# Retention input projections of row groups two to four by Strassen's seven half-block products

## The chip, the cores and the metric

The kernel runs on one core of a Trainium2 chip. The metric is device time in microseconds of one execution. Five engines work side by side from their own instruction queues: TensorE (PE; its weight loads are listed as PEld), VectorE (DVE), ScalarE (ACT), GpSimd (POOL) and SyncE (SP), which here issues every DMA. Matrix products read SBUF and accumulate in PSUM banks of 128 x 512 float32.

## The reference, cut to what matters

A decoder trunk of two layers over 2048 tokens of width 1024 in float32: one gated retention layer, then one sliding-window attention layer whose keys and values come from the residual stream after the first.

```python
def retention_layer(x, g_norm, w_in, w_out, sin, cos):
    proj = rmsnorm(x, g_norm) @ w_in                 # 1024 -> 1024 + 1024 + 2048 + 2048
    q, k, v, gate = jnp.split(proj, [D_MODEL, 2 * D_MODEL, 2 * D_MODEL + RET_V_TOTAL], axis=-1)
    q = theta_shift(q.reshape(b, s, RET_HEADS, RET_QK_DIM), sin, cos)
    k = theta_shift(k.reshape(b, s, RET_HEADS, RET_QK_DIM), sin, cos)
    v = v.reshape(b, s, RET_HEADS, RET_V_DIM)
    o = rms(retention(q, k, v))                      # chunks of 128, state 256 x 512 per head
    o = o.reshape(b, s, RET_V_TOTAL) * jax.nn.silu(gate)
    return x + o @ w_out

def step(state, inp):                                # inside retention, one chunk
    scores = jnp.einsum('bihd,bjhd->bhij', qc, kc) * intra_decay[None]
    intra = jnp.einsum('bhij,bjhe->bihe', scores, vc)
    inter = jnp.einsum('bihd,bhde->bihe', qc, state) * q_decay[None, :, :, None]
    new_state = state * chunk_decay + jnp.einsum('bjhd,bjhe->bhde', kc * k_decay, vc)
```

The attention layer then computes shared keys and values, gated attention with sinks and a bias by distance, and its output product.

## The kernel before

**Precision.** Every large product is made of three matmuls: each operand is split into a rounded high part (type fp32r, ACT) and the rest (DVE), and high x high, high x low and low x high are added in PSUM. `wload` (L100) brings a 128 x 1024 piece of weights through three rotating buffers `raw`, casts it (`whi`, L114) and subtracts (`wlo`, L116: DVE in the retention layer, POOL in the attention layer).

**Tiling.** Tokens are taken in four row groups of 512 (`T`), with four heads each: 16 units `(g, h)`, in this order. `main(u)` makes the projections of a unit from the group's split rows `xhi`, `xlo`, by three calls of `proj` (L119): queries and keys together (feature-major, 512 columns of tokens), values, gate. Each runs over eight blocks of 128 features for four PSUM banks, and all four banks of the pool `pp` turn over at its end (`evac_qk` rotates by position, `evac_v` splits the values, `evac_g` applies the gate). `ret(u)` runs four chunks of retention: scores (`sc_r`, L351), transposed keys (`kt_r`), state update (`dl_r`, L388 to L390), output (`o_r`), normalising and gating, transposing back (`ot_r`). The states of the four heads stay in SBUF (`S32`). `out_a(u)` multiplies a unit's output with its rows of the output weights in eight feature blocks (`pp_ao`) and adds them to the group's residual rows `x1`, which stay in SBUF for the group's four heads (L444), and are stored to `xmid` with the last head.

**Order.** The loop before `phase_b` interleaves `main(u + 1)` with `ret(u)` (`drive`, two steps to one), then emits `out_a(u)`. The order of emission is the priority; a scheduler orders the instructions of each engine before the run, pulling ready work forward into gaps. At run time each queue is strictly in order: an instruction that waits holds up what stands behind it, on SP too.

**Around it.** `row_stats` gets the scales of a group's rows, which are applied to the values and inside the norm and not to the rows. `bias_rows` (L204 on, run once after unit 0's projections) makes the bias by distance for 16 heads and stores 128 copies of each to `bdr` in DRAM (L216). `prep` brings rows to the attention layer. That layer's output product `out_b` loads each residual block, adds and stores it (`res`, L680 to L682).

Of the kernel before, what the change touches and what calls it, by code (L numbers as in the profile page):

```python
# [12 lines left out]
F32 = mybir.dt.float32  # L13
# [3 lines left out]
ALU = mybir.AluOpType  # L17
# [37 lines left out]
def tile_yoco(ctx, tc, x, x_t, w_a, wo_a, w_kv, w_b, wo_b, ag, kvg, bg, kng, qng,  # L55
# [8 lines left out]
    xtp = ctx.enter_context(tc.tile_pool(name="xtp", bufs=2))  # L64
# [13 lines left out]
    # the first function's table, loaded while the first rows come in  # L78
# [8 lines left out]

    def bank(name, tag="rr"):
# [11 lines left out]
    def wload(src, cols, name, kscale=None, key=None):  # L100
        """A piece of weights, split. Its rows scaled: in its first use, which stores it."""
# [17 lines left out]
    def proj(src, nk, xhi, xlo, feat, evac, name, kscale=None, key=None, cols=512, before=None):  # L119
        kn = 1024 // cols  # L120
        bk = [pp.tile([P, 512], F32, tag="pp", name=f"pp_{name}_{m}") for m in range(4)]
# [26 lines left out]
    def xt_tiles(name):  # L148
        mk = lambda hl, j: xtp.tile([P, KT // 2, T], F32R, tag=f"x{hl}", name=f"x{hl}_{name}_{j}")
        return [mk("hi", 0), mk("hi", 1)], [mk("lo", 0), mk("lo", 1)]  # L150

    def row_stats(g):
        """Mean squares + eps of the rows of a group, [P, MT], and their roots' inverses."""
        ss = small.tile([P, MT], F32, tag="ssx", bufs=2, name=f"ssx_{g}")
        r = small.tile([P, MT], F32, tag="rx", bufs=2, name=f"rx_{g}")
        for m in range(MT):
            xin = wp.tile([P, D], F32, tag="raw", bufs=3, name=f"xin_{g}_{m}")
            nc.sync.dma_start(xin, x[(g * MT + m) * P : (g * MT + m + 1) * P, :])
            junk = small.tile([P, D], BF16, tag="junk", bufs=1, name=f"jx_{g}_{m}")
            nc.scalar.activation(junk, xin, AF.Square, accum_out=ss[:, m : m + 1])  # L160
            if m == MT - 1:
                nc.gpsimd.tensor_scalar(ss, ss, 1.0 / D, EPS, op0=ALU.mult, op1=ALU.add)
                nc.gpsimd.tensor_tensor(r, ss, neghalf[:, :MT], op=ALU.pow)
            yield ss, r

    def stats(g, tiles, tag):
        """The scales of a group's rows, in every partition: [P, T]."""
# [16 lines left out]
    def prep(g, rb):  # L184
        """The normalised, transposed rows of a group, split."""
        xhi, xlo = xt_tiles(f"b{g}")
        for kp in range(KT // 2):
# [3 lines left out]
            hi, lo = (t[kp // 2][:, kp % 2 * 2 : kp % 2 * 2 + 2, :] for t in (xhi, xlo))  # L191
# [10 lines left out]
    bdr = dram.tile([QH, P, 384], F32, name="bdr")  # L202

    def bias_rows():  # L204
        """Bias by distance, a one-hot product; a copy for each query row, so that
        rows 384 wide read at a stride of 383 give bias[i, head, j]."""
# [5 lines left out]
        bp = pp.tile([P, 512], F32, tag="pp", name="biasp")  # L212
# [3 lines left out]
        nc.sync.dma_start(bdr, bsb.unsqueeze(1).to_broadcast([QH, P, 384]))  # L216
# [3 lines left out]
    # ------------------------------------------------------------ retention layer  # L220
    def phase_a(pa):
        cst = pa["const"]
        p1, p2, vp, gp = pa["p1"], pa["p2"], pa["v"], pa["g"]
# [9 lines left out]

        def main(u):
            g, h = units[u]
            n = f"a{u}"
            if h == 0:
                xt = xt_tiles(n)

# [614 lines left out]
```

## Time and profile before

| | |
|---|---|
| time, median of 3 runs | 2584.8 us (2583.43 to 2589.42) |
| span of the profiled execution, first to last instruction | 2580.5 us |
| mean granted TensorE clock | 0.990 |
| bytes moved by DMA | 283.29 MB, mean 110 GB/s |
| retention layer, its first to its last projection or output product | about 8 to 1737 us |

The profile is one execution of the program, and its span leaves out what lies before the first and behind the last instruction. A group of instructions carries its line, engine, operation, output and inputs, shapes and count, then its busy time and the mean duration of one in ns, then the idle time of the engine ahead of it with what ended that idle time. Matmuls overlap, so that their durations add up to more than the time they take.

### The profile page before, as it was taken

The numbers are of one execution on the slowest core, as the hardware profiler recorded it, in microseconds if no ns is written. First come the engines' busy times: TensorE is split into PE (matmuls) and PEld (weight loads), VectorE is DVE, ScalarE is ACT, GpSimd is POOL, SyncE is SP. The second block draws the span as 40 slices with busy tenths as digits, with TensorE's granted clock in tenths as the row PEclk, the third lists the DMA queues.
The fourth block names the chain that finished last, engine by engine and source line by source line (L and its number), as shares of the span: only waits on it lengthen the run. The fifth ranks groups of instructions, "written<-read, shape, count | busy, mean of one in ns | idle before, by whom it ended". The sixth has DMA issues, their size and how long they took to land.

```text
span 2580.5 us, 31642 instructions
## 1 busy us (share of the span) xinstructions
PE 2513.0 (97%) x12098; PEld 2046.3 (79%) x12098; DVE 1490.4 (58%) x2653; ACT 1017.3 (39%) x1859; POOL 487.0 (19%) x429
## 2 busy tenths in 40 slices
PE   8699999999999999999999999989999999999998
PEld 6588888888888888888888888878767777877887
DVE  4255455454555545546455454567876677777766
ACT  4242333333324333233333332334544454555553
POOL 1000000020000020000002000033325364363350
PEclk9899999999999999999999999999999999999999
DMA  5532223243223243222324222227332342333323
GB/s 173 106 115 82 90 81 116 85 141 114 80 81 110 85 155 106 82 82 82 123 74 143 90 74 82 86 90 255 126 122 91 131 142 83 139 124 113 127 102 107
DMA packets 92228, 283.29 MB, mean 110 GB/s; under 512 B 10763, under 2 KB 17068, under 8 KB 92076
## 3 DMA queue, kind: packets, MB, share of 16 engines
q1 hardware_dynamic: 92076, 281.27, 32.3%
q8 instruction: 95, 1.56, 0.2%
q14 instruction: 57, 0.47, 0.1%
HBM read 242.43 MB, written 38.80 MB: 109 GB/s over the span
## 4 chain that ended last, share of the span: by engine, by line
PE 89%; DVE 4%; DMA 3%; issue 2%; ACT 1%; POOL 1%; SPq 0%; POOLq 0%; ACTq 0%; DVEq 0%
PE pp_ao L136 4%; PE pp_ao L138 4%; PE pp_ao L137 4%; PE o_t L663 2%; PE s_t L626 2%; PE pp_bo L136 2%; PE pp_bo L138 2%; PE pp_bo L137 2%; PE pT_t L647 2%; DMA raw_a1qk<-in_w_a 1%; PE sc_r L351 1%; PE ot_r L422 1%; PE dl_r L388 1%; PE dl_r L389 1%; PE o_r L398 1%
## 5 line engine op out<-in xcount | busy, mean ns | idle before, releaser
L94 POOL TENSOR_SCALAR r_o_r<-sso_r,es_a 128x1 f32<-128x1 f32 x64 | 30.6, 478 | 1288.0 <-ACT jo_r L416 1288.0
L136 PE MATMUL pp_ao<-ohi_r,whi_ao 128*128 128x512 f32 x512 | 203.3, 400 | 0.0
L137 PE MATMUL pp_ao<-olo_r,whi_ao 128*128 128x512 f32 x512 | 202.6, 396 | 0.0
L116 DVE TENSOR_TENSOR wlo_ao<-raw_ao,whi_ao 128x1024 fp32r<-128x1024 f32 x64 | 78.4, 1225 | 211.1 <-ACT whi_ao L114 210.8
L138 PE MATMUL pp_ao<-ohi_r,wlo_ao 128*128 128x512 f32 x512 | 199.5, 396 | 0.0
L637 ACT ACTIVATE P_t<-P_t,nm_t 128x256 f32<-128x256 f32 (+1 forms) x256 | 127.5, 499 | 144.6 <-DVE nm_t L629 143.6
L114 ACT CAST whi_ao<-raw_ao 128x1024 fp32r<-128x1024 f32 x64 | 67.1, 1048 | 192.4 <-PE pp_ao L137 53.7
L629 DVE CUSTOM_DVE_ANT_0 P_t<-s_t,bias,nsnk 128x256 f32<-128x256 f32 (+1 forms) x256 | 114.9, 469 | 32.6 <-PE s_t L626 31.9
L138 PEld LDWEIGHTS pp_ao<-ohi_r,wlo_ao 128*128 128x128 f32 x512 | 96.4, 188 | 22.9
L137 PEld LDWEIGHTS pp_ao<-olo_r,whi_ao 128*128 128x128 f32 x512 | 96.5, 188 | 22.7 <-issue 0.2
L136 PEld LDWEIGHTS pp_ao<-ohi_r,whi_ao 128*128 128x128 f32 x512 | 96.7, 189 | 22.4 <-issue 0.2
L468 ACT CAST Shi_r<-S 128x512 fp32r<-128x512 f32 x120 | 70.4, 618 | 109.2 <-PE o_r L398 65.7
L409 DVE SCALAR_TENSOR_TENSOR S<-S,dl_r 128x512 f32<-128x512 f32 x112 | 73.2, 682 | 61.3 <-PE dl_r L390 61.2
L626 PE MATMUL s_t<-kst,qst_b 128*128 128x256 f32 (+1 forms) x512 | 100.5, 297 | 6.1 <-DVE nm_t L629 4.6
L626 PEld LDWEIGHTS s_t<-kst,qst_b 128*128 128x128 f32 x512 | 82.8, 192 | 29.7 <-DVE nm_t L629 7.4
L469 DVE TENSOR_TENSOR Slo_r<-S,Shi_r 128x512 fp32r<-128x512 f32 x120 | 78.1, 686 | 38.0 <-ACT Shi_r L468 37.8
L643 DVE TENSOR_SCALAR P_t<-P_t,den_t 128x256 f32<-128x256 f32 (+1 forms) x256 | 92.7, 425 | 1.9
L136 PE MATMUL pp_bo<-ohi_t,whi_bo 128*128 128x512 f32 x224 | 88.7, 401 | 3.6 <-DVE gate_b L590 3.6
L137 PE MATMUL pp_bo<-olo_t,whi_bo 128*128 128x512 f32 x224 | 88.2, 394 | 0.0
L116 POOL TENSOR_TENSOR wlo_bo<-raw_bo,whi_bo 128x1024 fp32r<-128x1024 f32 x28 | 71.1, 2542 | 86.5 <-ACT whi_bo L114 64.5
L138 PE MATMUL pp_bo<-ohi_t,wlo_bo 128*128 128x512 f32 x224 | 86.4, 394 | 0.0
L416 ACT ACTIVATE jo_r<-o_r 128x512 bf16<-128x512 f32 x64 | 38.0, 593 | 101.5 <-PE o_r L401 101.3
(867 smaller groups left out, 7308.0 us busy)
## 6 DMA issues: line engine op xcount, KB each, us to landing
raw_ao<-in_wo_a SPq DMA_DIRECT2D x64, 512.0 KB, 3.2
res<-xmid SPq DMA_DIRECT2D x56, 256.0 KB, 2.8
raw_bo<-in_wo_b SPq DMA_DIRECT2D x28, 512.0 KB, 3.2
xin<-in_x SPq DMA_DIRECT2D x16, 512.0 KB, 3.6
xraw_b<-xmid SPq DMA_DIRECT2D x16, 512.0 KB, 3.4
xmid<-res SPq DMA_DIRECT2D x32, 256.0 KB, 2.6
xraw_a<-in_x_t SPq DMA_DIRECT2D x12, 512.0 KB, 3.2
x_r<-in_x_t SPq DMA_DIRECT2D x12, 512.0 KB, 5.3
```

The lines of the kernel that those rows point to most:

```text
L114: nc.scalar.copy(hi, raw)
L116: eng.tensor_tensor(lo, raw, hi.bitcast(F32), op=ALU.subtract)
L136: nc.tensor.matmul(o, hi[:, kk, sl], xh, start=st, stop=False)
L137: nc.tensor.matmul(o, hi[:, kk, sl], xl, start=False, stop=False)
L138: nc.tensor.matmul(o, lo[:, kk, sl], xh, start=False, stop=sp)
L409: nc.vector.scalar_tensor_tensor(S32[h][:, d, :], S32[h][:, d, :], gamC[h], dl[d], op0=ALU.mult, op1=ALU.add)
L468: nc.scalar.copy(hi, S32[h][:, d, :])
L469: nc.vector.tensor_tensor(lo, S32[h][:, d, :], hi.bitcast(F32), op=ALU.subtract)
L626: nc.tensor.matmul(o, qst[m][:, h, :], kst[:, kv * 2 + hl, kb + b0 : kb + 2, :], start=hl == 0, stop=hl == 1)
L629: nc.vector.tensor_tensor_reduce(out=pt[:, j, :w], in0=o, in1=bias[:, kv * GQ + h, b0 * P :], scale=-1.0, scalar=nsv[:, h : h + 1], op0=AL ...
L637: nc.scalar.activation(pt[:, j, :w], pt[:, j, :w], AF.Exp, scale=-1.0, bias=nm[:, c : c + 1], accum_out=den[:, c : c + 1])
L643: nc.vector.tensor_scalar_mul(pt[:, j, :w], pt[:, j, :w], den[:, c : c + 1])
```

## The change

**Half blocks.** The rows of a group are cut into four blocks A11, A12, A21, A22: 256 tokens by 512 features each. The weights of a head are cut likewise: 512 features by the columns of q (j = 1) and k (j = 2), and by those of v and gate. From sums of blocks,

```
S1 = A21 + A22   S2 = S1 - A11   S3 = A11 - A21   S4 = A12 - S2
T1 = B12 - B11   T3 = B22 - B12  T2 = B11 + T3    T4 = B21 - T2
C11 = A11 B11 + A12 B21
C22 = A11 B11 + S2 T2 + S1 T1 + S3 T3
C12 = A11 B11 + S2 T2 + S1 T1 + S4 B22
C21 = A11 B11 + S2 T2 + S3 T3 + A22 T4
```

seven products replace eight. The first group (units 0 to 3, `PLAIN = 4`) keeps the plain products; the other twelve units use `strassen`, once for q/k and once for v/gate. Sums run in PSUM: products 1, 3, 5, 6 are added up in banks `a`, which ACT copies out after 1, 3 and 5; products 2, 4 and 7 go to banks `b`, and DVE adds the copies to them.

**Sums in advance.** The weight sums T are the same for all groups: `stage_sums` forms them on POOL during the first group and stores them to DRAM. `stage_rows` forms the row blocks and sums of the next group, now with the rows' scale applied, and stores them; `load_block` reads them back and splits them. One step of such work is taken at each step of `main` (`behind`, `step`).

**Room in SBUF.** The residual rows no longer stay there: `out_a` loads each block from `x_t` or `xmid` and stores it back for every head, through two buffers `res`. The heads' states go through DRAM (`S_d`) between groups. `bias_rows` stores 16 rows once and then copies them from DRAM to DRAM, one DMA for each head, two after each unit from the fifth loop step on. The split rows' tiles are quarters, not halves. `pp` has two banks each of two kinds instead of four of one.

**The rest.** `drive` takes four steps of `main` to one of `ret` (before: two). Transposed keys are made in the first two chunks. The row scales of the last three groups are in the rows, and no longer in the values and gate.

```diff
+PLAIN = 4
+SX = ("A11", "A12", "S2", "S3", "S1", "S4", "A22")
+ST = ("T2", "T3", "T1", "T4")
...
-    pp = ctx.enter_context(tc.tile_pool(name="pp", bufs=4, space=bass.MemoryType.PSUM))
+    pp = ctx.enter_context(tc.tile_pool(name="pp", bufs=2, space=bass.MemoryType.PSUM))
...
-        nc.sync.dma_start(bdr, bsb.unsqueeze(1).to_broadcast([QH, P, 384]))
+        nc.sync.dma_start(bd, bsb)
+        yield
+        for h in range(QH):
+            nc.sync.dma_start(bdr[h], bd[h].partition_broadcast(P))
+            yield
...
+        def stage_rows(g):
...
+            nc.tensor.matmul(rp, ones, dg, start=True, stop=True)
...
+            for k in range(KT // 2):
+                t = [stp(f"xst_{g}_{k}_{j}") for j in range(2)]
+                for j in range(2):
+                    kk = k + KT // 2 * j
+                    nc.sync.dma_start(t[j], x_t[g, kk // 2, :, kk % 2, :])
+                    nc.vector.scalar_tensor_tensor(t[j], t[j], ags[:, kk : kk + 1], rb, op0=ALU.mult, op1=ALU.mult)
...
+                nc.gpsimd.tensor_tensor(s1, a21, a22, op=ALU.add)
+                nc.gpsimd.tensor_tensor(s2, s1, a11, op=ALU.subtract)
+                nc.gpsimd.tensor_tensor(a21, a11, a21, op=ALU.subtract)
+                nc.gpsimd.tensor_tensor(s4, a12, s2, op=ALU.subtract)
+                for n, v in zip(SX, (a11, a12, s2, a21, s1, s4, a22)):
+                    nc.sync.dma_start(d[n][:, k, :], v)
+                yield
...
+        def load_block(g, n):
+            raw = wp.tile([P, KT // 2, H], F32, tag="raw", bufs=3, name=f"xb_{g}_{n}")
+            nc.sync.dma_start(raw, st["rows", g][n])
...
+            nc.scalar.copy(hi, raw)
+            nc.vector.tensor_tensor(lo, raw, hi.bitcast(F32), op=ALU.subtract)
...
+        def stage_sums(h):
...
+            for c, (src, dst) in enumerate(pieces):
+                b = [[stp(f"b{h}_{c}_{i}{j}") for j in range(2)] for i in range(2)]
...
+                        nc.sync.dma_start(view(b[i][j]), src[i][j])
+                (b11, b12), (b21, b22) = b
+                nc.gpsimd.tensor_tensor(b22, b22, b12, op=ALU.subtract)
+                nc.gpsimd.tensor_tensor(b12, b12, b11, op=ALU.subtract)
+                nc.gpsimd.tensor_tensor(b11, b22, b11, op=ALU.add)
+                nc.gpsimd.tensor_tensor(b21, b21, b11, op=ALU.subtract)
+                for t, dt in zip((b11, b22, b12, b21), dst):
+                    nc.sync.dma_start(dt, view(t))
+                yield
...
+        def strassen(n, src, feat, evac, after=None):
+            nb = 1 if feat else 2
+            a = [pbank("a", f"pp_{n}a{f}") for f in range(nb)]
...
+            def copy(p):
+                r[p] = [p1.tile([P, 512], F32, tag="r", bufs=4, name=f"r_{n}_{p}{f}") for f in range(nb)]
+                for f in range(nb):
+                    nc.scalar.copy(r[p][f], a[f])
+            def result(i, j, part=None, bk=None):
...
+                    nc.vector.tensor_tensor(r[part][f], r[part][f], bk[f], op=ALU.add)
+                    evac(i, j, f, r[part][f])
+            for p in range(7):
+                if p in (1, 3):
+                    b = [pbank("b", f"pp_{n}b{p}{f}") for f in range(nb)]
+                dst = b if p in (1, 3, 6) else a
+                xh, xl = st["block", SX[p]]
+                pieces = src(p)
+                kn = KT // 2 // len(pieces)
+                for i, w in enumerate(pieces):
+                    hi, lo = wload(w, 1024 // kn, f"{n}_{p}{i}")
+                    for kk, f in [(kk, f) for f in range(2) for kk in range(kn)]:
...
+                        if feat:
+                            o = dst[0][:, f * H : (f + 1) * H]
+                            mm = ((hi[:, kk, sl], xh[:, k, :]), (hi[:, kk, sl], xl[:, k, :]), (lo[:, kk, sl], xh[:, k, :]))
+                        else:
+                            o = dst[f]
+                            mm = ((xh[:, k, sl], hi[:, kk, :]), (xh[:, k, sl], lo[:, kk, :]), (xl[:, k, sl], hi[:, kk, :]))
...
+                if p in (0, 2, 4):
+                    copy(p)
+                if p == 1:
+                    result(0, 0, 0, b)
+                elif p == 4:
+                    result(1, 1, 4, b)
+                elif p == 5:
+                    result(0, 1)
+                elif p == 6:
+                    result(1, 0, 2, b)
...
         def out_a(u):
...
+            def load(f):
+                t = p1.tile([P, T], F32, tag="res", bufs=2, name=f"res_a{u}_{f}")
+                nc.sync.dma_start(t, x_t[g, f // 2, :, f % 2, :] if h == 0 else xmid[g][f // 2][:, f % 2, :])
+                res.append(t)
+            load(0)
+            for f in range(KT):
+                if f + 1 < KT:
+                    load(f + 1)
...
+                t = res[f]
                 nc.vector.tensor_tensor(t, t, ps, op=ALU.add)
-                if h < RH - 1:
-                    return
-                if f % 2:
-                    nc.sync.dma_start(xmid[g][f // 2], x1[f // 2])
+                nc.sync.dma_start(xmid[g][f // 2][:, f % 2, :], t)
...
-            drive(tc, main(u + 1), ret(u), 2, 0)
+            drive(tc, main(u + 1), ret(u), 4, 0)
+            for _ in itertools.islice(bias, 2 if u >= RH else 0):
+                pass
```

More of the change, by code (lines that the diff above doesn't have):

```diff
@@ L120, in proj @@
         kn = 1024 // cols
-        bk = [pp.tile([P, 512], F32, tag="pp", name=f"pp_{name}_{m}") for m in range(4)]
+        bk = [pbank("ab"[m // 2], f"pp_{name}_{m}") for m in range(4)]
         for kp in range(nk // kn):
@@ L148, in xt_tiles @@
     def xt_tiles(name):
[L149 to L164, printed above, removed]
+        return [[xtp.tile([P, 2, T], F32R, tag=f"x{hl}{j}", name=f"x{hl}_{name}_{j}") for j in range(4)]
+                for hl in ("hi", "lo")]
     def stats(g, tiles, tag):
@@ L228, in phase_a, with step, stp @@
         ep = cst.tile([P, RH], F32, name="ep")
-        S32 = [cst.tile([P, 2, DV], F32, name=f"S{h}") for h in range(RH)]
+        S_d = [dram.tile([P, 2, DV], F32, name=f"Sd{h}") for h in range(RH)]
         units = [(g, h) for g in range(NG) for h in range(RH)]
         nu = len(units)
-        st = {"x1": []}
+        st = {}
+        behind = []
+        def step():
+            if behind and next(behind[0], "end") == "end":
+                behind.pop(0)
+        def stp(name):
+            return p1.tile([P, T], F32, tag="st", bufs=6, name=name)
```

397 lines of the change are left out of this document (267 added, 130 removed).

## The prediction

> **What bounds the kernel now.** The first view is the page's table of busy time, the second a table of windows; the windows' columns are the window, its length, then PE, PEld (weight load), DVE, ACT and POOL busy with instruction counts, the granted clock, the DMA share and GB/s.
>
> ```profile
> span 2580.5 us, 31642 instructions
> PE 2513.0 (97%) x12098; PEld 2046.3 (79%) x12098; DVE 1490.4 (58%) x2653; ACT 1017.3 (39%) x1859; POOL 487.0 (19%) x429
> ```
>
> ```profile
> 88.00:126.00 38.00, 18.21 (x76) 14.74 (x75) 8.15 (x10) 5.07 (x9) 1.60 (x2) 0.73 0.84 136
> 295.00:400.00 105.00, 105.00 (x480) 86.42 (x480) 53.28 (x68) 33.23 (x47) 5.36 (x11) 1.00 0.25 86
> 502.00:1650.00 1148.00, 1148.00 (x5235) 945.36 (x5234) 599.34 (x766) 401.74 (x581) 97.97 (x144) 1.00 0.29 100
> 1760.00:2580.00 820.00, 795.30 (x4282) 632.39 (x4280) 587.93 (x1496) 410.20 (x989) 327.32 (x197) 0.99 0.36 125
> 848.30:1273.30 425.00, 425.00 (x1937) 349.97 (x1936) 221.78 (x285) 149.32 (x217) 36.23 (x54) 1.00 0.29 101
> ```
>
> From 502 to 1650 us TensorE is never idle: there the retention layer costs what its matmuls cost, and only fewer or shorter ones shorten it. One row group (four units, 848 to 1273) takes 425.0 us, so a unit takes 106.3. In the attention layer (1760 on) TensorE idles 24.7 of 820 us, or 3.0%, with DVE busy 72%. The window 88 to 126 is the exception, taken up below.
>
> The unit of cost is the distance between starts, not the busy duration, as matmuls overlap. In the timeline (start, duration, engine, line), first and last of eleven 512-column matmuls in a row, then the 256-column ones of the last output product:
>
> ```profile
> 899.70 0.39 PE L141 MATMUL pp_a8v<-wlo_a8v,xhi_a 128*128 128x512 f32 x1
> ...
> 901.97 0.39 PE L142 MATMUL pp_a8v<-whi_a8v,xlo_a 128*128 128x512 f32 x1
> ```
>
> ```profile
> 2575.92 0.28 PE L717 MATMUL pp_l<-ohi_t,xlo_last 128*128 128x256 f32 x1
> 2576.04 0.28 PE L715 MATMUL pp_l<-ohi_t,xhi_last 128*128 128x256 f32 x1
> 2576.16 0.28 PE L716 MATMUL pp_l<-olo_t,xhi_last 128*128 128x256 f32 x1
> ```
>
> 2.27 us over ten steps is 0.227 us for 512 columns; for 256 columns it is 0.120, which is 0.53 and not 0.50 of it.
>
> **Term 1, the products.** A unit's q/k projection is 8 x 4 x 3 = 96 matmuls of 512 columns, 96 x 0.227 = 21.8 us. By seven half blocks it is 7 x 4 x 2 x 3 = 168 matmuls of 256 columns, 168 x 0.120 = 20.2: 1.6 us less. The value and gate projections together are 192 of 512 columns; they become 7 x 4 x 2 x 3 = 168 of 512, 24 x 0.227 = 5.4 us less. A unit gains 7.1 us, the twelve units from the second row group on **-85 us**.
>
> By the Trainium skill ("TensorE: Matmul & The Clock Gate", Back-to-back issue gap) the distance is columns / 2.4 + 2.5 ns, 216 and 109 ns. By it q/k would gain 2.4 us a unit and the term be -93; the rows above have 227 and 120, and no run here shows the smaller ones.
>
> **Term 2, the bias rows.** The 128 copies per head go out in 16 DMAs from DRAM to DRAM, two per unit after the fourth, in place of one of 3 MB from 16 partitions. The wait view (who waited for whom, total, times, longest), the DMA issues with median time to landing, and the timeline after the wait:
>
> ```profile
> PE pp_a1qk L136 <- ACT whi_a1qk L114: 19.8, 1, 19.8
> ```
>
> ```profile
> bdr<-bsb SPq DMA_DIRECT2D x1, 3072.0 KB, 34.6
> raw_a0qk<-in_w_a SPq DMA_DIRECT2D x4, 512.0 KB, 4.9
> raw_a1qk<-in_w_a SPq DMA_DIRECT2D x4, 512.0 KB, 14.2
> ```
>
> ```profile
> 122.20 0.63 PE L136 MATMUL pp_a1qk<-xhi_a,whi_a1qk 128*128 128x512 f32 x1
> 122.63 0.63 PE L137 MATMUL pp_a1qk<-xlo_a,whi_a1qk 128*128 128x512 f32 x1
> ```
>
> The big store holds up unit 1's weights: TensorE waits 19.8 us and then runs some nine matmuls at 0.43 instead of 0.227 (1.8 us). Both go: **-21.5 us**. The 16 small stores carry the same 3 MB over eight units, 0.4 MB in each, against 10.7 MB that a unit moves now (101 GB/s x 106 us); I cost them at nothing, between 0 and the old 21.5.
>
> **Term 3, small additions on TensorE.** Each of three groups spreads its rows' scale by one product with ones:
>
> ```profile
> 1719.94 1.02 PE L179 MATMUL rp<-st,ones 128*128 128x512 f32 x2
> ```
>
> That is **+3 us** in all. At the start, unit 0's first step over k needs two weight pieces, not one; bounds 0 and one landing (4.9), taken **+2**.
>
> **Term 4, what the other engines get.** Per unit the weight pieces go from 12 + 4 to 21 + 4. Prices (line, engine, operation, shapes, count; then total us, mean ns):
>
> ```profile
> L116 DVE TENSOR_TENSOR wlo_a11g<-raw_a11g,whi_a11g 128x1024 fp32r<-128x1024 f32 x4 | 4.9, 1226 | 7.2 <-ACT whi_a11g L114 7.1
> L444 DVE TENSOR_TENSOR x_r<-x_r,pp_ao 128x512 f32<-128x512 f32 x32 | 21.9, 686 | 6.2 <-PE pp_ao L138 6.0
> L424 ACT CAST ohi_r<-ot_r 128x512 fp32r<-128x512 f32 x16 | 9.3, 584 | 22.1 <-PE ot_r L422 22.0
> L114 ACT CAST whi_a11g<-raw_a11g 128x1024 fp32r<-128x1024 f32 x4 | 4.2, 1049 | 8.1 <-PE pp_a11v L142 4.5 <-PE pp_a11g L142 3.6
> ```
>
> A new group is 425 - 28.3 = 397 us. DVE: 36 more pieces (44 us), 36 partial-sum adds at the price of L444 (25), 7 row blocks split (9): 222 + 78 = 300, 75%. ACT: 36 pieces (38), 36 bank copies (21), 7 blocks (7): 215, 54%. Neither binds, but DVE reaches the load that it has in the attention layer. DMA: 43 MB now, plus pieces 18.9, residual 12.6 (32 reads and 32 writes of 0.26 MB less 8 transfers of 0.52), states 4.2, row blocks 7.3: 86 MB, 217 GB/s, share 0.29 x 2.15 = 0.62. SP issues about 25 weight, 16 residual, 2 state and 12 row DMAs a unit; at 0.33 us each, 18 of 99 us.
>
> ```profile
> 992.63 0.33 SPq L106 DMA_DIRECT2D raw_a9v<-in_w_a  x1
> raw_ao<-in_wo_a SPq DMA_DIRECT2D x64, 512.0 KB, 3.2
> res<-xmid SPq DMA_DIRECT2D x56, 256.0 KB, 2.8
> xmid<-res SPq DMA_DIRECT2D x32, 256.0 KB, 2.6
> ```
>
> Two waits are new. After product 5 of a q/k round TensorE may not add into its bank until ACT has copied it: 0.58 us and two handovers, about 0.9, or 11 us over 12 units if nothing covers it (for v/gate the first bank is done six matmuls, 1.4 us, earlier, which covers the copy). The cover is the retention's own 100 or so matmuls a unit, already placed where banks turn over between two projections:
>
> ```profile
> 904.72 1.95 PE L351 MATMUL sc_r<-q_a,k_a 128*128 128x128 f32 x16
> ```
>
> The residual store waits for its add and the load two blocks later waits for that store, both on SP, with later weight loads behind them. The attention layer's output product has this very chain, and its cost shows on both queues:
>
> ```profile
> 2102.26 0.32 SPq L682 DMA_DIRECT2D xmid<-res  x1
> 2104.33 0.32 SPq L680 DMA_DIRECT2D res<-xmid  x1
> ```
>
> ```profile
> 2114.58 0.69 DVE L681 TENSOR_TENSOR res<-res,pp_bo 128x512 f32<-128x512 f32 x1 [2.46 <-DMA res<-xmid]
> ```
>
> Store to next load 2.1 us, landing 2.8, add 0.7 and handovers make 6 to 7 us for two blocks, 3.0 to 3.5 each, against 12 x 0.227 = 2.7 on TensorE. Four banks let TensorE run ahead.
>
> The stalls of the Strassen part lie between 0 (the same retention at full TensorE now) and 3.0% of 1191 us, 36 (the attention layer, with the same residual chain and DVE load). I take two thirds, **+24 us**, as the new load resembles the latter more. A gain below zero is excluded there: TensorE has no idle time left to win.
>
> The first four units also form the weight sums on POOL: 24 pieces of four operations, with 50 MB of traffic. One such operation is 1.3 us, 125 us in all, and DVE's splits stretch beside it:
>
> ```profile
> 941.03 1.56 DVE L116 TENSOR_TENSOR wlo_a9qk<-raw_a9qk,whi_a9qk 128x1024 fp32r<-128x1024 f32 x1 [0.24 <-ACT whi_a9qk L114]
> 948.42 1.23 DVE L116 TENSOR_TENSOR wlo_a9qk<-raw_a9qk,whi_a9qk 128x1024 fp32r<-128x1024 f32 x1 [4.82 <-ACT whi_a9qk L114]
> ```
>
> ```profile
> 940.21 1.30 POOL L456 TENSOR_TENSOR acc<-acc,sqx 128x512 f32<-128x512 f32 x1 [6.47 <-ACT sqx L451]
> ```
>
> 0.33 us on 96 occasions is 32 us of DVE in four units where it is half busy (53 of 105); I cost it at nothing, at worst 3.0% of 420 us, 13. The Trainium skill ("SBUF — State Buffer", Who interferes with whom) says that of a DVE instruction with two SBUF inputs and a GpSimd one reading SBUF the later blocks fully. By it DVE would lose up to 125 us, stand near 80%, and the 13 us would be due. The row stretches a 1.23 us split by 0.33, not by 1.3, so the trace agrees in kind and not in size.
>
> The attention layer keeps its instructions; its row tiles come in quarters rather than halves, so their splits may start earlier: nothing, at best -5, the waits of its first key product:
>
> ```profile
> PE pp_b0kv L140 <- ACT whi_b0kv L114: 3.3, 2, 1.9
> PE pp_b0kv L141 <- DVE wlo_b0kv L116: 1.3, 2, 0.8
> ```
>
> **Sum.** -85 - 21.5 + 3 + 2 + 24 = -77.5. Against the span: 2580.5 - 77.5 = 2503. The median, 2584.8, is 4.3 above that span; with this kept, **2507 us**.
>
> **The rivals.**
> (a) Everything is covered: without the 24 us, 2483. For it: no idle in 1148 us now; against it: DVE at 75% and twice the DMA. Chance 0.22.
> (b) The residual chain binds: with 3.4 us per block instead of 2.7, 0.68 x 8 x 15 units = 82 us on 2483: 2565. For it: the 2.46 us wait above; against: four banks and fillers. Chance 0.17.
> (c) Weight supply binds, the slower side. Three raw buffers make one round each of issue 0.33, landing 3.2, cast 1.05, split 1.23 and handovers, about 6.5 us, one piece every 2.2; a product uses a piece in 2.7 to 2.9, and 25 pieces a unit need one every 4.0. It decides from a round of 12.7 us (25 x 12.7 / 3 = 106, the old unit), a landing near 9 us. At 13 us a unit is 108.3, 12 x 9.1 = 109 more than 2483: 2592. For it: weights did land in 14.2 us when the DMA share was 0.84; against: the share here comes to 0.62. Chance 0.07.
> (d) The change does less than it says, the 256-column matmuls bound by a weight load each. The load's own row in that product, mean 191 ns:
>
> ```profile
> L716 PEld LDWEIGHTS pp_l<-olo_t,xhi_last 128*128 128x128 f32 x64 | 12.2, 191 | 1.6 <-issue 0.8 <-DVE olo_t L668 0.8
> ```
>
> At that distance q/k costs 32 us a unit and the result is about 2650. The rows 0.120 apart contradict it. Chance 0.02.
>
> The forecast itself has 0.52: 2507, give or take 15. Below 0.2% (5 us) a change can't be told from none on this kernel. Faster: 0.52 + 0.22 + 0.17 = 0.91; same: 0.02 of (c), a landing just at the deciding point; slower, the rest of (c) with (d): 0.07. The range runs from (a) with the early splits and a cheap start, 2474, to near (b), 2562.
>
> **What would show it.** Starts 0.120 apart in the seven q/k products and 0.227 in the others, with groups two to four near 397 us plus stalls: term 1. No wait of TensorE over 3 us on unit 1's weights: term 2. PE idle between 0 and 3% of the second to fourth group, put down to bank copies, residual adds or weight casts: term 4. Adds of the output product 3 us or more apart with PE idle behind them: (b). Casts waiting for DMA and landings near 9 us: (c). The forecast fails most likely in the 24 us, if queues of SP or DVE run in an order that real transfers don't keep up with.

## The result, and the profile after

The changed kernel takes **2626.7 us** (median of 4 runs, 2619.9 to 2635.6) where the kernel before takes 2584.1 beside it: a ratio of 1.016, 95% interval 1.014 to 1.019, so 43 us slower. The prediction, 2507 us, has the wrong sign, and the time lies outside its range.

The page of the changed kernel, its table of busy time and the DMA total of its third part:

```profile
span 2624.0 us, 35069 instructions
PE 2477.4 (94%) x12680; PEld 2040.2 (78%) x12680; DVE 1736.2 (66%) x2957; ACT 1176.7 (45%) x2076; POOL 680.6 (26%) x537
...
DMA packets 188858, 477.57 MB, mean 182 GB/s; under 512 B 21723, under 2 KB 38796, under 8 KB 188684
```

TensorE is busy for 36 us less (2513.0 to 2477.4), and the span is 43 longer: it waits more. The windows (columns as in the prediction) say where:

```profile
460.00:884.00 424.00, 406.30 (x2122) 341.86 (x2121) 292.93 (x378) 202.00 (x286) 56.30 (x58) 0.98 0.64 209
884.00:1314.00 430.00, 411.05 (x2137) 348.09 (x2136) 296.20 (x386) 202.13 (x287) 52.94 (x58) 0.98 0.62 201
1314.00:1740.00 426.00, 408.00 (x2148) 347.31 (x2147) 287.53 (x377) 196.00 (x286) 34.22 (x46) 0.98 0.53 176
1740.00:2624.00 884.00, 842.43 (x4486) 670.70 (x4484) 619.85 (x1536) 427.24 (x1010) 352.07 (x214) 0.98 0.38 127
```

```profile
0.00:460.00 460.00, 409.64 (x1795) 332.21 (x1796) 239.68 (x281) 149.33 (x209) 185.05 (x162) 0.96 0.74 249
```

Groups two to four, where TensorE was never idle, now have 18 to 19 us of idle time each, at a clock of 0.98, with about the load on DVE, ACT and DMA that the prediction had worked out (293 us, 202 us and a share of 0.64 in the second group, where it had 300, 215 and 0.62). The first row group has 50 us of idle time, where the kernel before has 33 (423.0 less 390.3):

```profile
0.00:423.00 423.00, 390.28 (x1752) 320.09 (x1753) 201.24 (x259) 143.38 (x199) 25.04 (x51) 0.98 0.37 111
```

Cut at the first product of a unit, with what the prediction's terms give for each stretch:

| stretch, us | before | predicted | after | missed by |
|---|---|---|---|---|
| start to unit 4 (first group) | 423.0 | 403.5 | 460.0 | 56.5 |
| unit 4 to the first key product (groups two to four) | 1316.2 | 1258.2 | 1309.3 | 51.1 |
| from there to the end (attention layer) | 841.3 | 841.3 | 854.7 | 13.4 |

The cut is a moment and not a share of the work. Priced by their steps, the matmuls ahead of unit 4 take 382.6 us in the kernel before, 391.2 in the changed one and 380.5 to 391.2 in the runs below, so a difference of less than some 10 us between the same stretch of two runs can be work that was moved.

The wait view names three causes: the residual's loads, the norm's root on POOL, and the loads of the weight sums.

```profile
DVE res_a L682 <- DMA res_a<-xmid: 89.0, 39, 5.1
DVE gate_a L625 <- POOL r_o_r L101: 69.1, 42, 13.3
POOL b L313 <- DMA b<-in_w_vg: 59.3, 12, 7.8
PE ot_r L628 <- DVE gate_a L625: 38.0, 13, 9.0
PE pp_ao L678 <- DVE res_a L682: 13.2, 3, 5.5
PE pp_b0kv L146 <- ACT whi_b0kv L120: 5.3, 1, 5.3
```

The kernel before waits for the root too, but never for long:

```profile
DVE gate_a L419 <- POOL r_o_r L95: 44.7, 56, 3.7
```

The first chain of it, in the timeline of the first group: ACT, which completes the root's input, then POOL, DVE and TensorE.

```profile
141.30 0.19 ACT L622 ACTIVATION_READ_ACCUMULATOR jo_r<-o_r 128x1 f32 x1
```

```profile
153.76 1.26 POOL L313 TENSOR_TENSOR b<-b,b 128x512 f32<-128x512 f32 x1 [7.31 <-DMA b<-in_w_vg]
155.10 1.26 POOL L314 TENSOR_TENSOR b<-b,b 128x512 f32<-128x512 f32 x1
156.35 0.26 POOL L100 TENSOR_SCALAR r_o_r<-sso_r,es_a 128x1 f32<-128x1 f32 x1
156.57 1.26 POOL L315 TENSOR_TENSOR b<-b,b 128x512 f32<-128x512 f32 x1
157.79 0.55 POOL L101 TENSOR_TENSOR r_o_r<-r_o_r,neghalf 128x1 f32<-128x1 f32 x1
```

```profile
158.37 0.75 DVE L625 SCALAR_TENSOR_TENSOR gate_a<-o_r,r_o_r,gate_a 128x512 f32<-128x512 f32 x1 [13.34 <-POOL r_o_r L101]
```

```profile
159.27 0.45 PE L628 MATMUL ot_r<-ident,gate_a 128*128 128x128 f32 x1 [8.95 <-DVE gate_a L625]
```

The norm's root, two operations of 0.26 and 0.55 us on 128 numbers, stands in POOL's queue behind sums of weights. Its input is there at 141.5, and it begins at 156.35: the sums ahead of it work, and one of them waits 7.31 us for its load. DVE waits 13.34 for the root, with weight splits behind it, and TensorE 8.95 for DVE. This was the theory; the rivals were the sums' 50 MB of traffic, POOL's added work as such, and, for the whole loss, the residual round trip and late weights.

### The profile page after: what moved, and what is told of

The parts are those of the page before. It is cut to its first block, busy times and chain, and to the rows that moved or that the text cites. A ratio compares the mean times of both kernels' runs of the same rounds, so it can differ in the third digit from the quotient of the medians.

```text
span 2624.0 us, 35069 instructions
## 1 busy us (share of the span) xinstructions
PE 2477.4 (94%) x12680; PEld 2040.2 (78%) x12680; DVE 1736.2 (66%) x2957; ACT 1176.7 (45%) x2076; POOL 680.6 (26%) x537
## 4 chain that ended last, share of the span: by engine, by line
PE 54%; DMA 15%; DVE 9%; issue 3%; ACT 3%; POOL 2%; SPq 1%; DVEq 0%; ACTq 0%; POOLq 0%
DMA xmid<-res_a 4%; DMA res_a<-xmid 2%; PE o_t L907 2%; PE s_t L870 2%; PE pT_t L891 2%; PE pp_bo L142 1%; PE pp_bo L144 1%; PE pp_bo L143 1%; PE pp_ao L678 1%; PE pp_ao L679 1%; PE pp_ao L680 1%; DVE res_a L682 1%; DVE xlo_b L185 1%; PE pp_a14va L361 1%; PE pp_a15va L361 1%
## 5 line engine op out<-in xcount | busy, mean ns | idle before, releaser
L100 POOL TENSOR_SCALAR r_o_r<-sso_r,ep 128x1 f32<-128x1 f32 x48 | 37.2, 775 | 781.0 <-ACT jo_r L622 781.0
L682 DVE TENSOR_TENSOR res_a<-res_a,pp_ao 128x512 f32<-128x512 f32 x128 | 87.8, 686 | 207.1 <-DMA res_a<-xmid 89.0
L625 DVE SCALAR_TENSOR_TENSOR gate_a<-o_r,r_o_r,gate_a 128x512 f32<-128x512 f32 x64 | 47.9, 748 | 69.3 <-POOL r_o_r L101 69.1
```

The lines of the kernel that those rows point to most:

```text
L682: nc.vector.tensor_tensor(t, t, ps, op=ALU.add)
```

## The experiments

Times are medians, ratios are against the kernel before on the same chip. "Changed" is the changed kernel, 2626.7 us. The kernel before took 2584.1 to 2586.7 us beside the runs, on several chips, so that a difference of 3 us between two runs tells nothing. "By the starts" means: from the distances between matmul starts, what exceeds the usual step, idle and half-clock time together.

### Parts taken out of the changed kernel

**More residual buffers.** `tag="res"`: `bufs=2` to `bufs=4`, `tag="st"`: `bufs=6` to `bufs=4`.

> The changed kernel with four residual buffers for the retention's output product instead of two (the staging buffers go from six to four to make room). Theory, residual round trip: each residual load waits until the store two blocks earlier has landed, VectorE waits for the load in order, and everything behind it is late; with four buffers most of the 85 us of TensorE stalls and half clock in row groups two to four goes (to about 35), VectorE's wait for residual loads falls from 133 us to under 50, and the time is about 2575. Rival, weight supply: pieces of weights arrive late under twice the DMA traffic; then the groups stay near 425 us each and the time within 10 us of 2627.

2631.0 us, ratio 1.018 [1.016, 1.020]: buffers alone bring nothing. That is the time which the rival, late weights, had forecast, but TensorE's waits for weight casts in groups two to four come to 9 us, and the additions' waits for landings went:

```profile
DVE res_a L682 <- PE pp_ao L680: 95.1, 70, 3.8
...
DVE res_a L682 <- DMA res_a<-xmid: 10.4, 6, 4.1
```

By the starts TensorE loses 77 us in groups two to four instead of 92. The stretch itself is only 4.8 us shorter (1309.3 to 1304.5), as 9 us of matmul work moved into it; the first group, with fewer buffers for the sums, lost 4.3 with that much less to do, and the attention layer 2.5.

**No residual round trip.**

```diff
-            load(0)
+            if h == RH - 1:
+                load(0)
...
-                if f + 1 < KT:
+                if h == RH - 1 and f + 1 < KT:
...
+                if h < RH - 1:
...
+                    nc.vector.tensor_copy(t, ps)
+                    yield
+                    continue
```

> The changed kernel without the residual's DMAs for the first three heads of each group: VectorE copies the product's bank into the same buffer instead of adding, so the output lacks those heads' sums; only the fourth head loads and stores. Residual round trip: row groups two to four fall from 424, 430 and 426 us to about 405 each and the time to about 2560. Weight supply: landings get shorter by the missing 75 MB only, the groups fall by less than 8 us each, the time stays above 2600.

2595.5 us, ratio 1.0044 [1.0029, 1.0059]: 31 us less than changed, between the two expectations. First group 445.9, groups two to four 1284.2. The traffic left out is 50 MB (477.6 to 427.2), not the 75 of the expectation. The round trip is one cost, and not the larger.

**Sums without their arithmetic.** The four `nc.gpsimd.tensor_tensor` lines of `stage_sums` are left out.

> The changed kernel with the weight sums' loads and stores but without their 96 GpSimd operations (the stored T blocks are plain blocks, so the output is not the reference's). Theory, GpSimd's queue: the small root of the retention's norm stands behind sums that wait for their loads, so that gate, transposes and TensorE wait; without the operations TensorE's 24 us of waits for the gate before 460 us go to under 5 and unit 4 starts near 435 instead of 460, the time about 2600. Rival, the sums' 50 MB of traffic in the first group: unit 4 still starts within 8 us of 460 and the time stays within 10 us of 2627.

2581.6 us, ratio 0.9988 [0.9978, 0.9997]: 45 us less, more than the theory's 27, and most of it where the sums are:

```profile
0.00:417.20 417.20, 398.60 (x1786) 324.54 (x1787) 214.22 (x276) 149.11 (x208) 38.74 (x66) 1.00 0.78 274
```

The DMA share is even higher (0.78 after 0.74), so the traffic isn't it. The edit frees SP's queue as well: in the changed kernel the sums' stores wait there for POOL for 87 us of the first group, with weight loads behind them. But TensorE's waits for weight casts in that group are the same, 14.3 us with the arithmetic and 14.6 without, while its waits for the gate fall from 22.4 us to 0.4. So the loss came by the root and not by late weights.

**No sums at all.**

```diff
-                    name = (None, None, "T2", "T3", "T1", None, "T4")[p]
-                    s = st["sums", h][job][name] if name else w[...]
+                    s = w[((0, 0), (1, 0), (0, 1), (1, 1), (0, 0), (1, 1), (0, 1))[p]]
...
-                behind.append(stage_sums(0))
...
-            if 1 <= u + 1 < RH:
-                behind.append(stage_sums(u + 1))
```

> The changed kernel without the weight sums, their loads, operations and stores (the products read plain blocks of the weights in place of T, so the output is not the reference's). Beside the run without the GpSimd operations alone (2581.6): if only GpSimd's queue mattered, 2576 to 2584; if the 50 MB of traffic in the first group cost as well, 2570 or less.

2585.7 us, ratio 1.0005 [0.9994, 1.0016]. With the traffic gone as well (50 MB) it is 4 us above the run that keeps it: the traffic costs nothing that these runs show.

**Neither.** The second and third edit together.

> Both leavings-out at once, no GpSimd operations in the sums and no residual DMA for three of four heads (wrong sums in both, so the output is not the reference's). If the two costs are apart, 45 and 31 us, the time is about 2551; if they overlap, 2565 or more. Either way it bounds what the products' saving of 85 us leaves beside the kernel before with new bias rows (2565): still over 2551 minus 85 would mean that bank copies, weight splits and the attention layer keep the rest.

2552.5 us, ratio 0.987 [0.986, 0.989]. The two costs add up: 31 + 45 = 76 predicted 2551.

**Sums on DVE.** `gpsimd` to `vector` in the four lines.

> The changed kernel with the 96 operations of the weight sums on VectorE instead of GpSimd (0.69 us each instead of 1.3, nothing left out). If the cost was the place in GpSimd's queue ahead of the norm's root, the first group falls from 460 to about 425 us and the time to about 2592. Rival: any engine in order that waits for the sums' loads holds up what is behind it, and VectorE has more behind it: 2625 or more.

2615.2 us, ratio 1.011 [1.009, 1.013], first group 446.3, TensorE's waits for the gate there 4.3 instead of 22.4 us. Between the two: the root is free, but now DVE's queue has operations that wait for loads (28.2 us for `b<-in_w_vg`, 26.3 for `b<-in_w_qk`), and 65 us of added work. Sums cost in either queue; how much of that is waiting and how much work, this run does not tell.

### Parts put into the kernel before

**The new bias rows alone.** The diff's lines of `bias_rows`, and `islice(bias, 2 if u >= RH else 0)` in the loop.

> The kernel before with the new bias rows alone: 16 rows stored once, then 16 DMAs from DRAM to DRAM, two after each unit from the fifth step on. Theory: the 3 MB store held up unit 1's weights; TensorE's wait of 19.8 us and the half clock behind it go, the time is 2584 - 21 = about 2563. Rival, the small stores only move the wait: the time stays within 5 us of 2584.

**2565.2 us**, ratio 0.992 [0.991, 0.994], as term 2 had it. Of the kernels that do the whole computation only the one with two kinds of banks besides (below) is as fast. In the profiled run the first group lost 27.4 us of its 423.0 and hardly idles any more, while the rest of the kernel got 9.3 longer:

```profile
0.00:395.70 395.70, 387.23 (x1751) 318.65 (x1752) 201.03 (x258) 143.35 (x200) 24.44 (x51) 1.00 0.33 110
```

**The room alone.** `PLAIN = 16`; `stage_sums` and `stage_rows` are never called.

> The changed kernel with plain products in all 16 units and no weight sums and no row blocks: what is left of the change is residual rows and states through DRAM, the new bias rows, quarter tiles and two kinds of banks. If making room costs by itself, the row groups two to four take about 435 us instead of 425, the attention layer 855 instead of 842, and the time is near 2600. If the room is free while weights are fetched at the old pace, the time is near that of the kernel before with new bias rows, 2565, within 8 us.

2610.4 us, ratio 1.010 [1.008, 1.013]: 45 us above the bias rows alone. The room that the products need costs half of what they save. The run also keeps the change's other order of work (`drive` at four to one, transposed keys early, weights of q and k in pieces of 256 columns), which no run takes apart from the room.

**The room without the residual round trip.** The same with the edit of the second run.

> Plain products throughout, with the changed kernel's tiles, banks and states in DRAM, no sums and no row blocks (2610 us with the residual through DRAM), and now without the residual's loads and stores for the first three heads of a group: their additions are left out. If the residual round trip costs the same 31 us whatever stands beside it: about 2579, most of it in the retention layer. If it costs only where the seven products load DVE and the queues as well: 2603 or more.

2597.4 us, ratio 1.0046 [1.0031, 1.0061]: the round trip costs 13 us here and 31 beside the seven products. Its price depends on what stands beside it; neither theory's number.

**Two kinds of banks.** `tag="pp"`, `bufs=4` becomes `tag="ab"[m // 2]`, `bufs=2`.

> The kernel before with the new bias rows (2565 us) and one thing more: the projections' four PSUM banks are of two kinds with two buffers each, as in the changed kernel. Both layers use them. Theory: the attention layer's 11 to 20 us, which every variant of the changed kernel loses against the kernel before, come from the banks: then the time is about 2580 and the attention stretch (from its first key product to the end) grows from 844 to 855 or more. Rival, the quarter tiles or something else that lies between the layers: 2565, give or take 4, and the stretch stays at 844.

2563.0 us, ratio 0.991 [0.990, 0.993]: 2 us below the kernel without them, so they cost nothing.

**Quarter tiles.** `xt_tiles` as in the changed kernel, banks as before.

> The kernel before with the new bias rows (2565 us) and the split rows' tiles in quarters, banks as before. If the quarters cost the attention layer its 11 to 20 us (the scheduler starts a group's rows earlier and puts their splits ahead of others): about 2580, attention stretch 855 or more. If not: 2565, give or take 4, or up to 5 less, as the prediction had it, with the stretch at 844 or below.

2581.9 us, ratio 0.998 [0.997, 0.999]: **17 us** for the shape of a buffer, 5.3 up to the first key product and 9.0 behind it in the profiled run. It is lost where a row group gives way to the next: from the first key product of the last group to its first query product 25.1 us, where the kernel with halves takes 19.1 (the two windows, one of each kernel):

```profile
2318.00:2343.10 25.10, 22.60 (x152) 18.71 (x151) 17.84 (x57) 12.87 (x35) 7.96 (x5) 0.93 0.38 136
```

```profile
2310.00:2329.10 19.10, 18.88 (x150) 17.12 (x149) 12.76 (x45) 9.79 (x31) 3.39 (x2) 1.00 0.45 151
```

**Quarters turned.**

```diff
+        turn = {"b1": 1, "b3": 1}.get(name, 0)
-        return [[xtp.tile([P, 2, T], F32R, tag=f"x{hl}{j}", ...) for j in range(4)]
+        return [[xtp.tile([P, 2, T], F32R, tag=f"x{hl}{j ^ turn}", ...) for j in range(4)]
```

> The kernel before with the new bias rows and quarter tiles (2582 us, where halves gave 2565), and now the quarters of every second row group of the attention layer change places within each half: new rows of a first quarter wait for the readers of the old second one, as whole halves did. If the quarters cost 17 us because a new group's rows and key products start earlier and are put ahead of others: back to 2567 to 2573, with some 6 us left at the first key product, which this doesn't change, and the attention stretch at 846 or less. If the number of tiles costs it in itself: 2580 or more.

2571.6 us, ratio 0.994 [0.992, 0.996], attention stretch 846.9 (844.2 with halves, 853.2 with quarters). The same stretch is back at 19.3:

```profile
2318.00:2337.30 19.30, 19.06 (x151) 17.14 (x150) 12.78 (x45) 9.82 (x31) 3.36 (x2) 1.00 0.43 151
```

10 of the 17 us come back by a later release, with the tiles as small as before: an order of work that starts the next group sooner is worse here. Most of the rest lies ahead of the first key product (7.2 us in this profiled run), where the turn changes nothing, and its cause was not looked for.

### Mending the sums and the residual

**Sums ahead, by half pieces.** Pieces of 256 columns, a pair's loads issued before the pair ahead is summed.

> The changed kernel (2627 us); the weight sums are formed in pieces of half the columns, and the loads of a pair of pieces are issued one step ahead of its operations, through the same six buffers. POOL's work and the bytes stay. If what costs 45 us is an operation that waits for its loads in POOL's queue with the norm's root behind it: POOL's waits for these loads fall from 59 us to under 20, the first group from 460 to about 425 us, and the time to about 2590. If it is POOL's 125 us of added work, whatever it waits for: the first group stays at 445 or more and the time at 2615 or more.

2670.4 us, ratio 1.033 [1.031, 1.035], first group 493. The numbers are those of the second theory, but not for its reason, so it is a miss of both: POOL's waits stayed (55.5 us on `b<-in_w_vg`), and TensorE waited on unit 0's gate weights. The wait, and in the timeline of SP the first issue of the stretch and the one that ended it:

```profile
PE pp_a0g L146 <- ACT whi_a0g L120: 23.7, 2, 20.1
```

```profile
49.88 0.81 SPq L313 DMA_DIRECT2D b<-in_w_qk  x2
...
78.65 0.38 SPq L112 DMA_DIRECT2D raw_a0g<-in_w_vg  x1
```

For 29 us SP issued nothing but the sums' small loads and stores, most of them 0.3 to 0.5 us each. The run tells nothing of POOL; it shows that SP's issue time is a price of its own.

**Sums ahead, in two sets of whole pieces.**

```diff
+                kind, bufs = (("st", STB), ("r", 4))[c % 2]
...
+            load(0)
+            yield
+            for c in range(6):
+                if c + 1 < 6:
+                    load(c + 1)
```

> The changed kernel (2627 us); the weight sums' pieces alternate between two sets of four buffers (the second is that of the bank copies, not in use in the first group), and a piece's loads are issued one step ahead of its operations. Same pieces, bytes and POOL work as in the changed kernel. If 45 us are lost because an operation that waits for its loads stands in POOL's queue ahead of the norm's root: POOL's waits for these loads fall from 59 us to under 20, the first group from 460 to 425 or less, the time to about 2590. If POOL's 125 us of work are enough for it: waits fall, and the first group stays at 445 or more, the time at 2612 or more. If the waits don't fall, the lead isn't what they depend on, and the run tells of that alone.

2615.1 us, ratio 1.011 [1.009, 1.013], 12 us less. Neither theory's figures came, and by the expectation's own words the run would tell of the lead alone: POOL still waits for loads (47 us on `b<-in_w_vg` in the first group, where it had waited 59). But, as seen only afterwards, it waits less often ahead of a root: DVE's waits for the root there fell from 39.6 to 14.0 us, TensorE's for the gate from 22.4 to 8.8, and the first group from 460 to 437.6, with nearly the same work on POOL (groups two to four took 12 us more in the profiled run, some 5 of them work that had stood ahead of the cut):

```profile
0.00:437.60 437.60, 403.34 (x1771) 326.61 (x1771) 233.17 (x270) 146.34 (x203) 178.22 (x156) 0.97 0.75 256
```

**And the residual's loads three blocks ahead**, four buffers.

```diff
-            load(0)
+            for f in range(3):
+                load(f)
             for f in range(KT):
-                if f + 1 < KT:
-                    load(f + 1)
+                if f + 3 < KT:
+                    load(f + 3)
```

> As the kernel with two sets of staging buffers, and the residual's loads issued three blocks ahead of their addition, through four buffers instead of one ahead through two (four staging buffers instead of six pay for them). If the 31 us of the residual round trip come from the short lead of its loads: the waits of the residual's additions for landings fall from 89 us to under 30 and the time is 25 us or more below that of the kernel with two sets alone. If they come from the 128 loads and stores in SP's queue and the additions themselves: within 8 us of it.

2589.1 us, ratio 1.0008 [0.9994, 1.0022]: 26 us less, as the theory of the lead had it. (The profiled run of this kernel is the fastest of its ten and that of the last kernel the slowest of its four, so that their stretches differ by 38 us in all.)

```profile
DVE res_a L696 <- PE pp_ao L694: 106.4, 73, 5.2
...
DVE res_a L696 <- DMA res_a<-xmid: 14.5, 8, 3.6
```

The additions now wait for their products. Groups two to four gained 17 us, about what four buffers alone had given them (15 by the starts); the first group gained 19 more, which four buffers alone had not, presumably as the root's waits still ruled there. It is at 418, with POOL busy for 181 us:

```profile
0.00:418.20 418.20, 394.98 (x1756) 322.31 (x1756) 238.03 (x269) 143.87 (x200) 180.70 (x156) 0.98 0.78 268
```

That is near the first group of the run without the sums' arithmetic (417.2, POOL 39). By the starts TensorE loses 25 us in it, where it lost 17 in that run and 58 in the changed kernel: of the sums' cost in this group POOL's work as such need not be more than 8 us. How far each of the two edits would go alone there was not run.

**With the quarters turned.**

> The changed kernel with the sums' loads a step ahead in two sets of buffers and the residual's loads three blocks ahead (together 2589 us), and the quarters turned in the attention layer. If the quarters' early start is what that layer loses: 2578 to 2582. If not: 2587 or more. Still above the kernel before with the new bias rows (2565) either way.

2574.2 us, ratio 0.9955 [0.9940, 0.9969], a little below the forecast: attention stretch 843.3 instead of 855.8. The three mends take 52 us off the changed kernel and make it faster than the kernel before, but not than that kernel with the new bias rows.

## Why the prediction was wrong

**Term 1 (-85 us) was right, to within some 7 us.** The steps are as forecast where TensorE is not disturbed, 0.84 us over seven in q/k and 2.49 over eleven in values (timeline of the changed kernel, first and last):

```profile
1013.74 0.28 PE L361 MATMUL pp_a9qb<-xlo_A,whi_a9q 128*128 128x256 f32 x1
...
1014.58 0.28 PE L361 MATMUL pp_a9qb<-xhi_A,wlo_a9q 128*128 128x256 f32 x1
```

```profile
1016.09 0.39 PE L361 MATMUL pp_a9va<-whi_a9v,xlo_A 128*128 128x512 f32 x1
...
1018.58 0.39 PE L361 MATMUL pp_a9va<-wlo_a9v,xhi_A 128*128 128x512 f32 x1
```

Over all units the median step is 0.120 in q/k, and 0.230 to 0.231 in values and gate, where the plain products have 0.227: by these medians a unit saves 6.5 us and not 7.1, and twelve save 78. The stretch agrees: from unit 4 to the first key product the time without idle and half-clock time is 1218 us, where the kernel before has 1305. Of these 87 us 8.6 are work that stands ahead of the cut in the changed kernel, which leaves 79, against 82 from terms 1 and 3. (The -93 that the prediction sets beside this term mixes two prices: with 0.216 us for the value and gate products too it is -91.)

**Term 2 (-21.5) was right in its sum, in part by luck**: the bias rows alone gave 19.8 (2565.2 against 2585.0). The first group gained 27.4 in the profiled run, more than the wait and the half clock behind it, and the rest of the kernel, with the bias product and the small stores that the term had at nothing, took 9.3 more.

**The first failed step: the sums on POOL "at nothing, at worst 13".** They cost 45 us. The step weighed what POOL's work takes from DVE's splits, and that was small: up to unit 4 DVE is busy for 239.7 us with the sums' arithmetic and 214.2 without, 25 us where the step had 32. What it didn't ask is what stands behind a waiting sum in POOL's own queue. It had asked that of SP. The kernel before has the norm's root on POOL, four times a unit.

The step's single row was also misread. The split at 941.03 was stretched by 0.33 us and not by 1.3 because only 0.48 us were left of the POOL operation beside it (940.21 and 1.30 long). In the changed kernel the operation that begins second takes over 2 us when it begins soon after the other, on either engine, where a split alone takes 1.23 and a sum 1.29:

```profile
53.62 1.29 POOL L315 TENSOR_TENSOR b<-b,b 128x512 f32<-128x512 f32 x1
53.76 2.23 DVE L122 TENSOR_TENSOR wlo_a0g<-raw_a0g,whi_a0g 128x1024 fp32r<-128x1024 f32 x1 [5.27 <-ACT whi_a0g L120]
```

```profile
163.97 1.22 DVE L122 TENSOR_TENSOR wlo_a1g<-raw_a1g,whi_a1g 128x1024 fp32r<-128x1024 f32 x1 [2.27 <-ACT whi_a1g L120]
164.18 2.17 POOL L314 TENSOR_TENSOR b<-b,b 128x512 f32<-128x512 f32 x1
```

(The Trainium skill, "SBUF — State Buffer", Who interferes with whom, lets the later of such two instructions wait in full. These rows agree, in size too.) Few met, though: of the 96 sums 22 began within a weight split, and 20 weight splits began within a sum and were stretched by 13 us together, far from the 125 that the prediction took as the most.

**The second: term 4, +24, "between 0 and 36".** From unit 4 to the first key product TensorE lost 92 us by the matmul starts (70 idle, 22 at half clock behind the waits), where the kernel before lost 11. The mechanisms were named, the size was off: 25 to 33 us of it are the residual round trip (the stretch goes from 1309.3 to 1284.2 without it, and by the starts 59 us are lost), which rival (b) had priced at 82; waits put down to bank copies took 12.1, 6.5 in q/k, of the 11 without cover, and 5.6 in values and gate, where the step had none; weight casts and splits took some 15. Waits for the gate took 15.6 more, 11 of them at the end of the layer, where the last unit's chain runs almost alone (4.9 in the kernel before). The bound from the attention layer's 3.0% counted idle time alone, and that layer has neither bank copies nor 25 weight pieces a unit beside its chain; no run shows which of these made the difference.

**The third: the attention layer's "nothing, at best -5".** Quarter tiles cost the kernel before 17 us, 9 of them behind the first key product in the profiled run; turning them took 12.5 off that stretch in the mended kernel. The sign was taken from the instruction (an earlier split can't hurt); what changes is the order of a whole stretch.

**The rivals.** (c), the slower side, was not what happened: the medians of the landings, by unit and source, are 3.1 to 8.2 us and mostly under 5, where (c) would decide from near 9, the share was 0.53 to 0.64, and casts were rarely late. The kernel is slower by a mechanism that had no rival, so the 7% for slower came from the wrong place. (d) is excluded by the steps above. The low end of the range, 2474, is 2 us below what its parts give (2483 - 5 - 2).

**The sum.** About -80 and -20 came. Against them stand 45 (sums), 31 (residual), 17 (quarters) and some 50 us that no run assigns: 2584 - 80 - 20 + 45 + 31 + 17 is 2577, and the kernel takes 2627. In the mended kernel such a part is still there: 2565 - 85 = 2480 would be the bias rows and the products alone, and it takes 2574. Of these 94 us the first group holds 26 and the idle and half-clock time of groups two to four 66 more than with the bias rows alone. How it divides among bank copies, weight pieces and the retention's own chain was not tried.

## What to carry to other kernels

Before work is put on an engine "with room", list what else is in its queue: one operation that waits for a load delays everything behind it, and the shortest and most urgent work (here a root of 0.8 us) pays. A saving that needs room must be charged for the room, measured alone: here 45 of 85 us, the order of work included, and 17 of them seem to go to a buffer's shape, which changed no more than when the next work could start. And when a stage's idle share is taken as the ceiling of new stalls, ask whether that stage has all the new waits: here 3.0% was forecast at most, and 4.6% came (60 of 1309 us by the busy time), with half-clock time besides.

## What the runs showed of the hardware that had not been expected

The step of a 512-column matmul depends on its place: 0.233 us in the retention layer's output product (0.232 by the median of the kernel before), where the plain projections take 0.227 and Strassen's value and gate products 0.230 to 0.231, by the median. No run shows why. First and last of twelve in a row of the output product, 2.56 us over eleven steps:

```profile
448.40 0.39 PE L678 MATMUL pp_ao<-ohi_r,whi_ao 128*128 128x512 f32 x1
...
450.96 0.40 PE L680 MATMUL pp_ao<-ohi_r,wlo_ao 128*128 128x512 f32 x1
```

A stall costs more than its length, which the prediction had priced in term 2 and not in term 4. Behind the wait that ended at 159.27, matmuls start 0.43 us apart instead of 0.23 until 162.3:

```profile
161.00 0.63 PE L148 MATMUL pp_a1g<-whi_a1g,xlo_a 128*128 128x512 f32 x1
161.43 0.63 PE L146 MATMUL pp_a1g<-whi_a1g,xhi_a 128*128 128x512 f32 x1
```

In the stretch of the root's waits, 126 to 209 us, the granted clock was 0.91:

```profile
126.00:209.00 83.00, 67.89 (x297) 54.91 (x296) 32.21 (x36) 22.37 (x30) 48.08 (x37) 0.91 0.82 276
```
